# Operand tiles 32 bytes longer in a fused decoder block: the same instructions on other SBUF addresses

## The chip, the cores and the metric

The kernel runs on one NeuronCore of a Trainium2 chip. The metric is the device time of one execution in microseconds. A profiled execution gives a trace with the start and the duration of each instruction on TensorE (PE, with its weight loads shown apart as PEld), VectorE (DVE), ScalarE (ACT), GpSimd (POOL) and of each DMA.

## The reference

One decoder layer on x of 512 tokens by 1024 channels, all in float32:

```
h = rms_norm(x, g_mix);  p = h @ w_in              # 1024 -> 7680 columns
q, fp, iv, go, bg, cg, xc, u, v, gates = split(p)
o_a = hgrn2_mix(q, fp, iv, go)                     # gated linear recurrence, 4 heads of 128
o_b = short_conv_mix(bg, cg, xc)                   # 3-tap causal convolution
o_c = spatial_gating_mix(u, v)                     # 128 x 128 causal token mixing
merged = sum_n sigmoid(gate_n) * (o_n @ w_branch[n])
x = x + merged @ w_o
x = x + square(relu(rms_norm(x, g_ffn) @ w_ff1)) @ w_ff2   # 1024 -> 4096 -> 1024
return rms_norm(x, g_final)
```

## The kernel before, in words

Activations lie feature-major: a tile has 128 features on the partitions and the 512 tokens (`S`) along the free dimension, 2048 bytes per partition. Weights come in tiles of 128 by 1024 float32, 4096 bytes per partition, that is eight stationary blocks of 128 columns.

**Split operands.** Each large product is made of three matmuls in the float32r type. Every operand is split into a rounded part `hi` (an ACT copy) and the rest `lo` (a DVE subtraction), and `mm3` (L88 to L91) issues hi·hi (L89), hi·lo (L90) and lo·hi (L91) into one PSUM accumulator. Each of these matmuls has its own weight load of 128 columns, also where two in a row use the same block.

**Tiles.** Three helpers give out the SBUF tiles that these matmuls read: `xslot` (L55, 16 tiles of 128 by 512 for the input and later the second norm's input), `zslot` (L58, 24 tiles of 128 by 512: recurrence, branch inputs, hidden rows of the feed-forward, the residual) and `hslot` (L61, 16 tiles of 128 by 1024: the recurrence's work tiles, the merged rows, the second feed-forward weight). Each of these tags has one buffer. The split weights `wh` and `wl` (L83, L84, L744, L745, L795, L796) have three buffers each. The raw weight lands by DMA in `raw` (L74, three buffers). `tmp` (L113, six buffers of 2080 bytes) is for elementwise work, and `ones_r` (L105) is a constant block of ones.

**Order of the work.** The program's order is written out by hand. `proj` units (24 matmuls each: eight blocks of the contraction times three) give the input projection; `v_mm` (L403) makes the spatial gate's input with x stationary and the weight moving; the recurrence's small float32 matmuls (L317 and others, 128 columns) stand between the units; `branch` (L517) and `full` (L627) give the branch maps and the output projection. Then the feed-forward alternates: four units of `full` on the first weight (96 matmuls, moving operand x, stationary wh and wl), and `ff2_mm` of the group before (96 matmuls, moving operand z, stationary h). The last group is done in two token halves with 256-column matmuls (`fin_mm`, L897), and the final norm follows. In two ways there are other pairings: at the start x is stationary for the value rows (L833), and `ones_mm` (L144 to L146) sums over partitions with `ones_r` stationary and two `tmp` tiles moving; that happens three times.

Weights are prefetched: `issue` starts the DMA into `raw`, `split_hi` (L740) and `split_lo` make `wh` and `wl` (or two h tiles) one unit or more ahead of their matmuls.

Of the kernel before, what the change touches and what calls it, by code (L numbers as in the profile page):

```python
# [8 lines left out]
F32R = mybir.dt.float32r  # L9
# [4 lines left out]
P = 128  # L14
S = 512
# [21 lines left out]
def trunk_kernel(ctx: ExitStack, tc, xT, w_f, w_t, w_bc, w_a, w_o, w_1, w_2, vecs, rows, w_sg, cst, lmask, out):  # L37
    nc = tc.nc
    cp = ctx.enter_context(tc.tile_pool(name="cp", bufs=1))
    wp = ctx.enter_context(tc.tile_pool(name="wp", bufs=3))  # L40
    rp = ctx.enter_context(tc.tile_pool(name="rp", bufs=1))
# [6 lines left out]
    def nm(s):  # L48
        uid[0] += 1
        return f"{s}_{uid[0]}"  # L50

    def ct(shape, name, dt=F32):
        return cp.tile(shape, dt, name=name, tag=name)

    def xslot(i, dt):  # L55
        return rp.tile([P, S], dt, tag=f"x{i}", name=nm("x"))

    def zslot(i, dt):  # L58
        return rp.tile([P, S], dt, tag=f"z{i}", name=nm("z"))

    def hslot(i, dt):  # L61
        return rp.tile([P, 2 * S], dt, tag=f"h{i}", name=nm("h"))

    def acc():
        return pa.tile([P, S], F32, tag="acc", name=nm("acc"))
# [4 lines left out]
    def tt(e, o, a, b, op):  # L70
        return e.tensor_tensor(out=o, in0=a, in1=b, op=op)  # L71

    def raw():
        return wp.tile([P, 2 * S], F32, tag="raw", name=nm("raw"))  # L74

    def split(src, hi, lo):
        act.activation(hi, src, AF.Copy)
        tt(dve, lo, src, f(hi), ALU.subtract)

    def load_w(dram):  # L80
        r = raw()
        nc.sync.dma_start(r, dram)
        hi = wp.tile([P, 2 * S], F32R, tag="wh", name=nm("wh"))  # L83
        lo = wp.tile([P, 2 * S], F32R, tag="wl", name=nm("wl"))  # L84
        split(r, hi, lo)
        return hi, lo

# [5 lines left out]
    def cs(k, n=P):  # L93
        return slice(k * n, (k + 1) * n)

    # constants
    vec = ct([P, V_N], "vec")
    cons = ct([P, C_N], "cons")
    ident = cons[:, C_ID:C_ID + P]
# [13 lines left out]
        return wp.tile([P, w], dt, tag="tmp", name=nm("tmp"), bufs=6)  # L113

    def rsqrt_cols(src, n, inv, eps, dst):
        """dst[:, :n] = (src * inv + eps) ** -0.5"""
        a = wp.tile([P, 4], F32, tag="ra", name=nm("ra"), bufs=4)
        dve.tensor_scalar(out=a[:, :n], in0=src, scalar1=inv, scalar2=eps, op0=ALU.mult, op1=ALU.add)
        tt(pool, dst[:, :n], a[:, :n], mhalf[:, :n], ALU.pow)
# [49 lines left out]
    units = []  # L169
# [5 lines left out]
    loads, when = [], {}  # L175
# [14 lines left out]
            return a  # L190
        return unit(w_f[j], mm, ev)

    # recurrence: decays, keys, queries
    def ev_f(h, a):
        kk[h] = zslot(2 * h, F32)
        A[h] = zslot(2 * h + 1, F32)
        hs = [hslot(h * 4 + i, F32) for i in range(4)]
        names = ("QA", "t1", "QB", "y", "q", "R", "go", "att")
        d = {n: hs[i // 2][:, cs(i % 2, S)] for i, n in enumerate(names)}
        heads.append(d)  # L200
        fp = d["QA"]
        tt(dve, fp, a, rb, ALU.mult)
        act.activation(kk[h], fp, AF.Sigmoid, scale=-1.0)
        act.activation(d["t1"], fp, AF.Abs)
        pool.memset(d["att"], 0.0)
# [55 lines left out]
            dve.tensor_scalar(out=d["y"], in0=d["y"], scalar1=al[:, h:h + 1], scalar2=cl[:, h:h + 1], op0=ALU.add, op1=ALU.max)  # L261
            tt(dve, A[h], d["y"], d["t1"], ALU.add)

    # recurrence: interactions at distance scale m = 2 ** l
    def halves(ap, m):
        v = ap.rearrange("p (b two m) -> p b two m", two=2, m=m)
        if m == 1:
            v = v[:, :, :, 0]
            return v[:, :, 0], v[:, :, 1]
        return v[:, :, 0, :], v[:, :, 1, :]  # L270
# [51 lines left out]
            mk = lm[:, cs(l)].unsqueeze(1).to_broadcast([P, 4, P])  # L322
            dve.copy_predicated(v4(d["att"]), mk, v4(d["ps"]))

    # recurrence: blocks of 128 through the state
    def far_prep(pair):
        for h in pair:
            d = heads[h]
            act.activation(d["y"][:, :3 * P], d["R"][:, :3 * P], AF.Exp)
            act.activation(d["t1"][:, P:], A[h][:, P:], AF.Exp)  # L330
        for h in pair:
            d = heads[h]
            tt(dve, d["QA"][:, :3 * P], kk[h][:, :3 * P], d["y"][:, :3 * P], ALU.mult)
            tt(dve, d["QB"][:, P:], d["q"][:, P:], d["t1"][:, P:], ALU.mult)
# [64 lines left out]
            zt[0][h] = (zslot(2 * h, F32R), zslot(2 * h + 1, F32R))  # L399
            split(d["t1"], *zt[0][h])  # L400

    # spatial gate
    def v_mm(j):  # L403
        def mm(w):
            if j == 0:
# [73 lines left out]
        zt[2][g] = (zslot(16 + 2 * g, F32R), zslot(17 + 2 * g, F32R))  # L479
        split(part["sv", g], *zt[2][g])  # L480

    # short convolution
    def ev_cg(c, a):
        y = tmp()
        part["cy"] = y
        tt(dve, y, a, rb2, ALU.mult)
# [18 lines left out]
        yield  # L505
        tt(dve, lo, y, f(hi), ALU.subtract)

    # gates, branch outputs, merge
    def ev_gate(d, n, a):
        g = tmp()  # L510
        part[n] = g
        tt(dve, g, a, rb, ALU.mult)
        act.activation(g, g, AF.Sigmoid)
# [19 lines left out]
        tt(dve, mt[:, S:], part[0], f(mt[:, :S]), ALU.subtract)  # L533
        mg.append((mt[:, :S], mt[:, S:]))

    # order of the units of tensor work
    for h in range(NH):
        proj(4 + h, lambda a, h=h: ev_f(h, a))
    for h in range(NH):
# [57 lines left out]
        at(pre, 19 + g, sg_split, g)  # L597
    at(pre, 21, go_sig)

    # output projection, residual, second norm  # L600
    x2, x2h, x2l = [], [], []

    def reload_x():
# [37 lines left out]
        ones_mm(part["c2"], part["qh"], part["ql"])  # L641

    def ffn_rows():
        """-2 * (mean square + eps) ** -0.5, on every partition"""
        a, r, t = tmp(), tmp(), tmp()
        act.activation(r, part["c2"], AF.Sqrt, scale=1.0 / D, bias=eps_c)
        dve.tensor_scalar(out=a, in0=part["c2"], scalar1=1.0 / D, scalar2=EPS, op0=ALU.mult, op1=ALU.add)
        dve.reciprocal(r, r)
        tt(pool, t, a, r, ALU.mult)
        tt(pool, t, t, r, ALU.mult)  # L650
        part["r2b"] = ct([P, S], "rb2")
        dve.scalar_tensor_tensor(out=part["r2b"], in0=t, scalar=-3.0, in1=r, op0=ALU.add, op1=ALU.mult)
# [1 line left out]
    def ffn_late():  # L654
        return [ev_1(i, held[i]) for i in range(3)]

    # feed-forward
    hid = {}

    def ev_1(i, a):  # L660
# [67 lines left out]
    order = [x for s in sorted(when) for x in when[s]]  # L728
# [10 lines left out]
    def split_hi(i):  # L739
        _, n, tiles = loads[i]  # L740
        if tiles:
            hi, lo = (hslot(t, F32R) for t in tiles)
        else:
            hi = wp.tile([P, 2 * S], F32R, tag="wh", name=nm("wh"))  # L744
            lo = wp.tile([P, 2 * S], F32R, tag="wl", name=nm("wl"))  # L745
        act.activation(hi[:, :n], raws[i][:, :n], AF.Copy)  # L746
        ws[i] = (hi, lo)

# [4 lines left out]

    held = []
    with tc.manual_schedule():
        # warm the tensor engine's clock and the activation tables while the first loads run
        dve.memset(ones, 1.0)
        pool.memset(mhalf, -0.5)
        nc.scalar.dma_start(vec, vecs)
# [2 lines left out]
        warm = acc()  # L762
        for i in range(WARM):
            pe.matmul(warm[:, :P], ones, ones, start=True, stop=True)

        # x: load, scale by the gain, split, sum of squares; the recurrence's value rows, token-major
        xr = [zslot(k, F32) for k in range(KD)]
        rw = []
        for k in range(KD):
# [17 lines left out]
        for k in range(KD + 1):  # L787
            if k < KD:
                hi = xslot(2 * k, F32R)
                lo = xslot(2 * k + 1, F32R)  # L790
                xh.append(hi)
                xl.append(lo)
                g = vcol(V_GMIX + k)
                if k % 2 == 0:
                    wh = wp.tile([P, 2 * S], F32R, tag="wh", name=nm("wh"))  # L795
                    wl = wp.tile([P, 2 * S], F32R, tag="wl", name=nm("wl"))  # L796
                c = cs(k % 2, S)
                iw.append((wh[:, c], wl[:, c]))
                if k == 0:
                    dve.tensor_copy(wh[:, c], rw[k // 2][:, c])  # L800
                    pieces = (slice(0, 256), slice(256, 512))
                else:
                    pieces = (slice(0, 512),)
                for h in pieces:
                    act.activation(hi[:, h], xr[k][:, h], AF.Copy, scale=g)
                if k > 0:
                    act.activation(wh[:, c], rw[k // 2][:, c], AF.Copy)
                for h in pieces:
                    dve.scalar_tensor_tensor(out=lo[:, h], in0=xr[k][:, h], scalar=g, in1=f(hi[:, h]), op0=ALU.mult, op1=ALU.subtract)
                tt(dve, wl[:, c], rw[k // 2][:, c], f(wh[:, c]), ALU.subtract)  # L810
                if k == 0:
                    act.activation(sq_tot, xr[k], AF.Square)
                else:
                    sq = tmp()
                    act.activation(sq, xr[k], AF.Square)
                    tt(pool, sq_tot, sq_tot, sq, ALU.add)
            if k == KD:
                cps = acc()
                col_sums(cps, sq_tot)
                rsqrt_cols(cps[:, :4], 4, 1.0 / D, EPS, rstd)  # L820
                dg = diag(rstd)
                dh = ones_hi(dg)
                dl = ones_lo(dg, dh)
            j = k - 1
            if j < 0:
                continue
            hi, lo = xh[j], xl[j]
            wh_, wl_ = iw[j]
            for rnd in range(3):
                for t in range(4):  # L830
                    lh = (hi, hi, lo)[rnd][:, cs(t)]
                    rh = (wh_, wl_, wh_)[rnd]
                    pe.matmul(a4[t], lh, rh, start=j == 0 and rnd == 0, stop=j == KD - 1 and rnd == 2)  # L833
            if j in (3, 5, 6):
                issue()
            if j == 5:
                split_hi(order[0])
                split_lo(order[0])
# [52 lines left out]
                fn(*a)  # L891
        prev[0](prev[1])

        # last group of the feed-forward, by token halves, and the final norm
        g = NG - 1
        n2 = S // 2

# [75 lines left out]
        warm = acc()  # L973
# [60 lines left out]
```

## Time and profile before

| | |
|---|---|
| median of 3 runs | 860.64 us (859.86 to 861.35) |
| span of the profiled execution | 859.3 us |
| instructions in the span | 10105 |
| PE busy | 847.2 us, 99% |
| PEld busy | 706.8 us, 82% |
| DVE / ACT / POOL busy | 473.6 / 322.3 / 140.4 us |
| mean DMA rate | 97 GB/s |

The profiled execution is known by its span alone, from its first to its last instruction; what lies around the span in a timed run is the difference to the median, 1.3 us. A matmul's duration in the trace runs from its start to its modelled end and overlaps the next one, so the pace of PE is read from the starts of successive matmuls, not from their durations.

### The profile page before, as it was taken

To read this page: it belongs to the slowest core of one execution; us is meant where nothing else is said; L and a number is where in the kernel's file an instruction comes from. 1 tells how busy PE (TensorE), PEld (TensorE's weight loads), DVE (VectorE), ACT (ScalarE), POOL (GpSimd) and SP (SyncE) were. 2 spreads that over 40 slices of the span, in tenths; PEclk is the share of its full clock that TensorE was granted. 3 is DMA by queue.
4 is the path that set the end of the run, shared out by engine and by line. 5 is a ranking of instruction groups with operands and counts; after the bars stand their busy time and mean duration, and the time that the engine had idled before them with its cause. 6 is when DMAs were issued, how large, how long until landed. Compare 5 with 4: busy or idle time off the path is not lost.

```text
span 859.3 us, 10105 instructions
## 1 busy us (share of the span) xinstructions
PE 847.2 (99%) x3990; PEld 706.8 (82%) x3990; DVE 473.6 (55%) x623; ACT 322.3 (38%) x491; POOL 140.4 (16%) x152
## 2 busy tenths in 40 slices
PE   8999899999999999999999999999999999999997
PEld 7888788888888888888888888888888888888896
DVE  7456989978564444544445458444444444444424
ACT  6567355354333232323223446232232323232222
POOL 4313455661210000000001310000000000000034
PEclk9999999999999999999999999999999999999999
DMA  8331222212122323232235234222223232322002
GB/s 302 118 99 50 84 88 75 74 50 98 50 75 86 110 86 111 86 96 100 86 110 208 92 131 149 96 98 98 98 98 98 98 98 98 98 91 90 17 1 99
DMA packets 26256, 83.59 MB, mean 97 GB/s; under 512 B 3040, under 2 KB 3424, under 8 KB 26208
## 3 DMA queue, kind: packets, MB, share of 16 engines
q1 hardware_dynamic: 26064, 82.91, 29.1%
q8 instruction: 31, 0.51, 0.2%
q14 instruction: 17, 0.14, 0.1%
q10 hardware_dynamic: 144, 0.03, 0.0%
HBM read 80.83 MB, written 2.10 MB: 97 GB/s over the span
## 4 chain that ended last, share of the span: by engine, by line
PE 91%; DVE 3%; ACT 3%; issue 2%; DMA 0%; SPq 0%; POOL 0%; DVEq 0%; ACTq 0%
PE acc L89 28%; PE acc L91 28%; PE acc L90 28%; PE acc L317 3%; PE acc L833 1%; DVE wl L71 1%; DVE h L71 1%; ACT h L248 1%; DVE h L261 0%; DMA z<-xT 0%; ACT wh L746 0%; ACT h L252 0%; PE acc L469 0%; PE acc L370 0%; DVE h L298 0%
## 5 line engine op out<-in xcount | busy, mean ns | idle before, releaser
L89 PE MATMUL acc<-x,wh 128*128 128x512 f32 x672 | 265.5, 395 | 0.0
L90 PE MATMUL acc<-x,wh 128*128 128x512 f32 x672 | 262.7, 391 | 0.0
L91 PE MATMUL acc<-x,wl 128*128 128x512 f32 x672 | 262.7, 391 | 0.0
L746 ACT ACTIVATE wh<-raw 128x1024 fp32r<-128x1024 f32 (+1 forms) x112 | 115.0, 1028 | 377.0 <-PE acc L90 247.4
L71 DVE TENSOR_TENSOR wl<-raw,wh 128x1024 fp32r<-128x1024 f32 (+1 forms) x118 | 151.4, 1284 | 24.9 <-ACT wh L746 24.8
L91 PEld LDWEIGHTS acc<-x,wl 128*128 128x128 f32 x672 | 126.2, 188 | 28.6
L89 PEld LDWEIGHTS acc<-x,wh 128*128 128x128 f32 x672 | 126.3, 188 | 26.5
L90 PEld LDWEIGHTS acc<-x,wh 128*128 128x128 f32 x672 | 126.3, 188 | 26.4
L71 DVE TENSOR_TENSOR z<-z,acc 128x512 f32<-128x512 f32 (+1 forms) x80 | 50.6, 634 | 109.8 <-PE acc L91 109.8
L89 PE MATMUL acc<-z,h 128*128 128x512 f32 (+1 forms) x288 | 105.5, 366 | 0.0
L90 PE MATMUL acc<-z,h 128*128 128x512 f32 (+1 forms) x288 | 105.2, 365 | 0.0
L91 PE MATMUL acc<-z,h 128*128 128x512 f32 (+1 forms) x288 | 105.2, 365 | 0.0
L71 POOL TENSOR_TENSOR tmp<-tmp,tmp 128x512 f32<-128x512 f32 (+1 forms) x27 | 31.5, 1166 | 218.6 <-DVE tmp L71 186.9
L662 DVE SCALAR_TENSOR_TENSOR tmp<-acc,rb 128x512 f32<-128x512 f32 x32 | 21.9, 690 | 76.0 <-PE acc L91 76.0
L71 DVE TENSOR_TENSOR tmp<-acc,rb 128x512 f32<-128x512 f32 x28 | 19.3, 691 | 80.5 <-PE acc L91 80.5
L89 PEld LDWEIGHTS acc<-z,h 128*128 128x128 f32 x288 | 54.3, 189 | 8.8
L90 PEld LDWEIGHTS acc<-z,h 128*128 128x128 f32 x288 | 54.3, 189 | 8.8
L91 PEld LDWEIGHTS acc<-z,h 128*128 128x128 f32 x288 | 54.3, 189 | 8.7
L917 POOL TENSOR_SCALAR z<-z,vec 128x256 f32<-128x256 f32 x12 | 5.8, 484 | 312.5 <-ACT tmp L911 312.5
L663 ACT ACTIVATE tmp<-tmp 128x512 f32<-128x512 f32 x32 | 20.1, 628 | 69.2 <-DVE tmp L662 69.2
L71 DVE TENSOR_TENSOR h<-raw,h 128x1024 fp32r<-128x1024 f32 x32 | 38.9, 1217 | 0.0
L89 PE MATMUL acc<-z,wh 128*128 128x512 f32 x96 | 37.8, 394 | 0.0
(184 smaller groups left out, 984.4 us busy)
## 6 DMA issues: line engine op xcount, KB each, us to landing
raw<-w SPq DMA_DIRECT2D x64, 512.0 KB, 3.3
raw<-w_f SPq DMA_DIRECT2D x52, 512.0 KB, 3.3
raw<-w_bc SPq DMA_DIRECT2D x8, 512.0 KB, 3.3
raw<-w_o SPq DMA_DIRECT2D x8, 512.0 KB, 3.3
z<-xT SPq DMA_DIRECT2D x15, 256.0 KB, 4.3
raw<-w_t SPq DMA_DIRECT2D x4, 512.0 KB, 3.3
raw<-w_a SPq DMA_DIRECT2D x8, 256.0 KB, 2.5
out<-x SPq DMA_DIRECT2D x8, 256.0 KB, 2.1
```

The source lines that it names most:

```text
L71: return e.tensor_tensor(out=o, in0=a, in1=b, op=op)
L89: pe.matmul(o, lh, rh, start=start, stop=False)
L90: pe.matmul(o, lh, rl, start=False, stop=False)
L91: pe.matmul(o, ll, rh, start=False, stop=stop)
L248: act.activation(d["t1"], d["t1"], AF.Exp, scale=-1.0)
L317: pe.matmul(ps[:, cs(b)], kl[:, cs(b)], qk[:, cs(b)], start=True, stop=True)
L662: dve.scalar_tensor_tensor(out=t, in0=a, scalar=0.0, in1=part["r2b"], op0=ALU.max, op1=ALU.mult)
L663: act.activation(t, t, AF.Square, scale=0.5)
L746: act.activation(hi[:, :n], raws[i][:, :n], AF.Copy)
L833: pe.matmul(a4[t], lh, rh, start=j == 0 and rnd == 0, stop=j == KD - 1 and rnd == 2)
L917: pool.tensor_scalar(out=xv, in0=xv, scalar1=vcol(V_GFIN + d), scalar2=0.0, op0=ALU.mult, op1=ALU.add)
```

## The change

Every tile of `xslot`, `zslot`, `hslot`, `wh` and `wl` is allocated eight float32 elements longer and used without its last eight. Nothing else is changed (removed comments are left out of the diff):

```diff
     def xslot(i, dt):
-        return rp.tile([P, S], dt, tag=f"x{i}", name=nm("x"))
+        return rp.tile([P, S + 8], dt, tag=f"x{i}", name=nm("x"))[:, :S]
 
     def zslot(i, dt):
-        return rp.tile([P, S], dt, tag=f"z{i}", name=nm("z"))
+        return rp.tile([P, S + 8], dt, tag=f"z{i}", name=nm("z"))[:, :S]
 
     def hslot(i, dt):
-        return rp.tile([P, 2 * S], dt, tag=f"h{i}", name=nm("h"))
+        return rp.tile([P, 2 * S + 8], dt, tag=f"h{i}", name=nm("h"))[:, :2 * S]
...
-        hi = wp.tile([P, 2 * S], F32R, tag="wh", name=nm("wh"))
-        lo = wp.tile([P, 2 * S], F32R, tag="wl", name=nm("wl"))
+        hi = wp.tile([P, 2 * S + 8], F32R, tag="wh", name=nm("wh"))[:, :2 * S]
+        lo = wp.tile([P, 2 * S + 8], F32R, tag="wl", name=nm("wl"))[:, :2 * S]
```

The last two lines stand in the same form in `load_w`, `split_hi` and the opening loop. On all five engines the instructions, their order and their waits are the same in both programs. What moves is where the tiles start in each partition. From the two built programs, start address modulo 256 bytes:

| tiles | before | after |
|---|---|---|
| wh, 3 buffers | 32, 32, 32 | 32, 64, 96 |
| wl, 3 buffers | 32, 32, 32 | 128, 160, 192 |
| x, 16 tiles | 96, all | 96, 128, 160, 192, 224, 0, 32, 64, and again |
| z, 24 tiles | 96, all | all eight multiples of 32, in turn |
| h, 16 tiles | 96, all | all eight multiples of 32, in turn |
| raw, 3 buffers | 96, all | 96, all |
| tmp, 6 buffers | 96, 128, 160, 192, 224, 0 | the same |
| ones_r | 224 | 224 |

Each matmul's stationary block starts a multiple of 512 bytes into its tile, so it has its tile's offset. Of the 3345 places where one 512-column float32r matmul follows another, the distance from a moving tile to the next stationary one, modulo 256, was:

| distance | 0 | 32 | 64 | 96 | 128 | 160 | 192 | 224 |
|---|---|---|---|---|---|---|---|---|
| before | 675 | 0 | 189 | 1 | 4 | 0 | 2474 | 2 |
| after | 552 | 282 | 502 | 253 | 577 | 254 | 626 | 299 |

## Rows read from the trace of the kernel before

**Rows 1.** The page, busy time, share and instructions; granted clock in 40 slices.
```profile
PE 847.2 (99%) x3990; PEld 706.8 (82%) x3990; DVE 473.6 (55%) x623; ACT 322.3 (38%) x491; POOL 140.4 (16%) x152
...
PEclk9999999999999999999999999999999999999999
```

**Rows 2.** The chain that ended last: shares by engine; pieces (start us, us, what).
```profile
PE 91%; DVE 3%; ACT 3%; issue 2%; DMA 0%; SPq 0%; POOL 0%; DVEq 0%; ACTq 0%
...
1.63 3.82 DMA z<-xT
...
49.18 3.38 issue
...
96.27 1.96 PE acc L317 x8
```

**Rows 3.** Timeline of PE, second then first product, first matmuls: start us, us, instruction.
```profile
583.25 0.39 PE L89 MATMUL acc<-z,h 128*128 128x512 f32 x1
...
604.78 0.39 PE L91 MATMUL acc<-z,h 128*128 128x512 f32 x1
605.00 0.39 PE L89 MATMUL acc<-x,wh 128*128 128x512 f32 x1
...
626.98 0.39 PE L89 MATMUL acc<-z,h 128*128 128x512 f32 x1
```

**Rows 4.** Timeline of PE, v_mm: first and last of its first 72 matmuls.
```profile
74.99 0.39 PE L89 MATMUL acc<-wh,x 128*128 128x512 f32 x1
...
91.56 0.40 PE L91 MATMUL acc<-wh,x 128*128 128x512 f32 x1
```

**Rows 5.** Timeline of PE, last group: first and last of 120 half-width matmuls.
```profile
823.67 0.28 PE L89 MATMUL acc<-z,h 128*128 128x256 f32 x1
...
837.95 0.28 PE L91 MATMUL acc<-z,h 128*128 128x256 f32 x1
```

**Rows 6.** Timeline of PE around the three `ones_mm`, from first row to last.
```profile
35.35 0.40 PE L91 MATMUL acc<-x,wl 128*128 128x512 f32 x1
...
36.75 0.39 PE L89 MATMUL acc<-x,wh 128*128 128x512 f32 x1
...
57.81 0.40 PE L91 MATMUL acc<-x,wl 128*128 128x512 f32 x1
...
58.97 0.39 PE L91 MATMUL acc<-x,wl 128*128 128x512 f32 x1
...
505.64 0.39 PE L90 MATMUL acc<-x,wh 128*128 128x512 f32 x1
...
507.01 0.39 PE L91 MATMUL acc<-x,wl 128*128 128x512 f32 x1
```

**Rows 7.** Groups of matmuls by line: count, busy us, mean ns, idle before.
```profile
L89 PE MATMUL acc<-x,wh 128*128 128x512 f32 x672 | 265.5, 395 | 0.0
...
L89 PE MATMUL acc<-z,h 128*128 128x512 f32 (+1 forms) x288 | 105.5, 366 | 0.0
...
L89 PE MATMUL acc<-z,wh 128*128 128x512 f32 x96 | 37.8, 394 | 0.0
...
L89 PE MATMUL acc<-h,wh 128*128 128x512 f32 x64 | 25.2, 394 | 0.0
```

**Rows 8.** Groups by form, DVE then ACT, 510 to 820 us.
```profile
L71 DVE TENSOR_TENSOR h<-raw,h 128x1024 fp32r<-128x1024 f32 x30 | 36.5, 1217 | 0.0
L71 DVE TENSOR_TENSOR wl<-raw,wh 128x1024 fp32r<-128x1024 f32 x27 | 32.9, 1219 | 1.0 <-ACT wh L746 1.0
...
L746 ACT ACTIVATE h<-raw 128x1024 fp32r<-128x1024 f32 x30 | 31.4, 1045 | 0.0
L746 ACT ACTIVATE wh<-raw 128x1024 fp32r<-128x1024 f32 x27 | 28.5, 1056 | 128.9 <-PE acc L90 93.8 <-DMA raw<-w 35.0
```

**Rows 9.** The page, DMA issues: count, KB each, us to landing.
```profile
z<-xT SPq DMA_DIRECT2D x15, 256.0 KB, 4.3
```

More of the change, by code (lines that the diff above doesn't have):

```diff
@@ L743, in split_hi @@
         else:
-            hi = wp.tile([P, 2 * S], F32R, tag="wh", name=nm("wh"))
-            lo = wp.tile([P, 2 * S], F32R, tag="wl", name=nm("wl"))
+            hi = wp.tile([P, 2 * S + 8], F32R, tag="wh", name=nm("wh"))[:, :2 * S]
+            lo = wp.tile([P, 2 * S + 8], F32R, tag="wl", name=nm("wl"))[:, :2 * S]
         act.activation(hi[:, :n], raws[i][:, :n], AF.Copy)
@@ L794, in trunk_kernel @@
                 if k % 2 == 0:
-                    wh = wp.tile([P, 2 * S], F32R, tag="wh", name=nm("wh"))
-                    wl = wp.tile([P, 2 * S], F32R, tag="wl", name=nm("wl"))
+                    wh = wp.tile([P, 2 * S + 8], F32R, tag="wh", name=nm("wh"))[:, :2 * S]
+                    wl = wp.tile([P, 2 * S + 8], F32R, tag="wl", name=nm("wl"))[:, :2 * S]
                 c = cs(k % 2, S)
```

## The prediction

> **What bounds the kernel now.** I read the page first. TensorE is busy for 99% of the span at a granted clock of nine tenths or more in every slice, that is at its 2.4 GHz level; DVE is busy for 55%, ACT for 38% [rows 1]. The chain that ended last is PE for 91%, DVE and ACT for 3% each [rows 2]. Its pieces show where PE is not the limit: a DMA of x at the start (3.82 us), and the stretch from 49.18 us, where a wait of 3.38 us opens a chain of ACT and DVE work, to 96.27 us, where the first masked products (L317) get the chain back to PE. From there to the last group of the feed-forward the chain is matmul after matmul. So the time after about 104 us, and that before 49 us once the inputs are there, is the number of matmuls times the pace of PE.
>
> The pace comes from the timeline. A matmul's duration (395 or 366 ns [rows 7]) is a modelled latency and says nothing of it; the starts do. In the second feed-forward product 96 matmuls start between 583.25 and 604.78 us: 95 intervals in 21.53 us, **226.6 ns** each. In the next block, the first product, 96 intervals lie between 605.00 and 626.98 us: **229.0 ns** [rows 3]. In v_mm, 71 intervals between 74.99 and 91.56 us: **233.4 ns** [rows 4]. All three stream 512 columns, which takes 213.3 ns at 2.4 GHz, and all load 128 new columns each time. The 256-column matmuls of the last group have 119 intervals in 14.28 us, 120.0 ns [rows 5]. From 120.0 to 226.6 the extra 256 columns cost 106.6 ns, the full clock's rate, so about 13 ns of each matmul do not depend on its length, and 2 or 7 ns come on top in two of the three kinds.
>
> What differs between the kinds is where their operands lie. In the second product moving and stationary tiles both start at 96 modulo 256: distance 0, 226.6 ns. In the first product the moving tile is at 96 and the stationary at 32: distance 192, 229.0 ns. In v_mm it is the other way round: distance 64, 233.4 ns. This is a correlation over three kinds of code, but a change of offsets touches just this, and that makes it the question of the forecast.
>
> **The change part by part.** No instruction, wait or DMA is added, removed or moved. What changes is the start address of what PE, ACT, DVE, POOL and some DMAs read and write.
>
> *TensorE, the counts.* Matmuls at distance 192: three lines of 672, 96 and 64 [rows 7], 2,496; 110 of them run in the 49 to 104 us stretch where PE has slack, so 2,386 count. At distance 0: three lines of 288 [rows 7], 864, of which 192 are half width. At distance 64: v_mm, in the slack stretch, and the opening matmuls, which mostly wait for loads; both at nothing. If the offsets slow PE under the cover of 49 to 104 us, the 3 us in which PE waits there shrink first; 110 and 96 matmuls by 2 ns are 0.4 us.
>
> *TensorE, the new pace.* Afterwards the eight distances occur 253 to 626 times each, and they change from matmul to matmul. The trace has three distances in steady state; their mean is (226.6 + 229.0 + 233.4) / 3 = 229.7 ns. Of changing distances it has three samples, the three `ones_mm`, whose two moving tiles lie at 128 and 160, at 0 and 224, and at 0 and 96, with a stationary block at 224. Around the first, six intervals take 1.40 us; around the second, five take 1.16 us; around the third, six take 1.37 us [rows 6]. That is 3.93 us for 17, **231.2 ns** on average, where 17 at 229.0 ns are 3.89 us. If the 0.04 us are put down to the nine pairs in these samples whose distance is not the usual one, a changed pair costs about 4 ns more, 233 ns. I take the middle of 229.7, 231.2 and 233: 231.2 ns. Two of the three samples hold moving tiles at 0 and one holds one at 128, and none of their stretches is quicker than the block around it, so nothing shown speaks for a gain from a round address.
>
> The sum: 2,386 x (231.2 - 229.0) = 5.2 us; 672 x (231.2 - 226.6) = 3.1 us; 192 half-width matmuls by the same 4.6 ns, since the 13 ns showed themselves independent of length, 0.9 us. Together 9.2 us. The ends: if every pair ran at the best pace shown, 2,386 x 2.4 = 5.7 us less; if every one ran at the worst steady pace, 2,386 x 4.4 + 864 x 6.8 = 16.4 us more.
>
> *ACT, DVE and POOL.* The subtraction of a weight takes 1217 ns with operands at 96, 96 and 96 and 1219 ns with 96, 32 and 32; the ACT copy 1045 ns from 96 to 96 and 1056 ns from 96 to 32 [rows 8]. These engines hardly see the offset, so nothing. If that were wrong by 1%, the cover is their idle time (DVE 45%) except in the 49 to 104 us stretch, where 1% of it is half a microsecond.
>
> *DMA.* The weights land in `raw`, which does not move. The x tiles land in z tiles that do move (15 transfers, 4.3 us each to landing [rows 9]); on the chain they are the 3.82 us at the start [rows 2]. The trace has no such transfer to another offset. A tenth of 3.82 us either way is 0.4 us; I take nothing, because the transfer's size and form stay.
>
> The profiled span is 859.3 us, 1.3 us under the median of the timed runs; the same remainder is taken for the changed kernel. 859.3 + 9.2 + 1.3 = **869.8 us**.
>
> **A rule weighed against the trace.** Three distances and three paces [rows 3, 4] suggest that weight load and moving stream meet somewhere. The Trainium skill, "TensorE: Matmul & The Clock Gate", Part 2, step 1, says the opposite: TensorE has two independent SBUF read ports, and loading the next weights takes no read bandwidth from the running matmul. By it the sum would be 0. The rows do not refute it, since distance and kind of code change together in them. It is the first rival.
>
> **The rivals.**
>
> *1. Offsets do not matter; the paces belong to the kinds of code.* For it: in v_mm x is stationary and the weight moves, and in the second product the roles are played by h and z; distance is not the only difference. Against it: the branch maps and the output projection, with z and h moving and wh stationary, are other code at distance 192, and their matmuls show 394 ns, the same as the first product's 395 rather than the second's 366 [rows 7]. Then nothing changes: 860.6 us. Also the form in which the change does not do what it says: the offsets move, but PE never sees them. Chance 0.14.
>
> *2. The distance of 192 is a bad one, and the spread averages it away (the other side).* If most of the eight distances behave like 0, the 2,386 matmuls fall towards 226.6 ns and the second product keeps its pace: 5.7 us less, 854.9 us; half of it, 857.8 us. It decides at the point where the mean of the eight distances lies under about 228.5 ns, today's mean. For it: the best pace shown is one of three. Against it: both others and the samples lie above. Chance 0.14.
>
> *3. The 13 ns are themselves a collision of tiles that all start alike modulo 256.* Then a spread would remove part of it from most matmuls. All of it would be 2,386 x 15.7 + 864 x 13.3 = 49 us, 812 us; half, 836 us. For it: it is there at each length. Against it: it is no larger at distance 0 than at 64, and the samples at 0 and 128 are not quicker. Chance 0.07. By the rule of the same page's section "Back-to-back issue gap" a warm matmul costs its columns at 2.4 GHz plus 2.5 ns, an estimate of 215.8 ns for 512 columns; the trace shows 226.6 at best, so that page leaves about 11 ns unexplained, and a rival that removes it would end near this one's lower end.
>
> *4. Changing distances cost more than steady ones.* The first sample has 26 ns over 229.0 in six intervals with three changed pairs, near 9 ns a pair; at 237.7 ns for all, the time would be 859.3 + 30.4 + 1.3 = 891 us. Chance of over 880 us: 0.07.
>
> **How the numbers follow.** The forecast, that the mean distance is worse than the two distances of today, has 0.58, with a range of its own from 863 to 877 us (229.7 to 233.4 ns). About 0.2% is what a measurement of this kernel can tell from no change, here 1.7 us or 0.5 ns a matmul. Slower by more: 0.58 + 0.07 = 0.65. Within: 0.14. Faster by more: 0.14 + 0.07 = 0.21. The range goes from rival 2 at its full, with a margin for the start, 853 us, to 880 us, a little past the worst steady pace (877); it leaves out rival 3 and the upper part of rival 4.
>
> **What would show it.** In the changed profile the block of 96 matmuls of the second product should take longer than 21.53 us, about 22.0, and the first product's about 22.2 instead of 21.98, with intervals that vary from block to block with the buffer of wh. If both blocks keep their lengths to 0.05 us, rival 1 is right. If the first product's block shrinks to 21.75 us while the second's stays, rival 2 is; if intervals near 215 ns appear, rival 3 is. DVE's and ACT's mean durations should stay within 1%, PE busy at 98 to 99%. The forecast is wrong in its ground if the pace of a matmul in the changed kernel does not follow its distance at all.

## The result and the profile after

| | before | after |
|---|---|---|
| median | 861.0 us (859.86 to 862.09, 4 runs) | 870.92 us (870.11 to 871.11, 4 runs) |
| ratio | | 1.0112, 95% interval 1.0099 to 1.0126 |
| span of the profiled execution | 859.3 us | 868.3 us |

The changed kernel is 1.1% slower; 869.8 us was forecast, in a range from 853 to 880. The page of the changed kernel, where rows 1 stand for before:

```profile
PE 857.2 (99%) x3990; PEld 706.1 (81%) x3990; DVE 473.9 (55%) x623; ACT 322.8 (37%) x491; POOL 140.6 (16%) x152
...
PEclk9999999999999999999999999999999999999999
...
PE 93%; DVE 3%; ACT 3%; issue 1%; DMA 0%; SPq 0%; POOL 0%; DVEq 0%; ACTq 0%
...
z<-xT SPq DMA_DIRECT2D x15, 256.0 KB, 4.6
```

PE's busy time grew by 10.0 us and nothing else's by more than half a microsecond. The granted clock stayed at its upper level. The timeline of PE shows the new pace, first in the blocks that rows 3 show (second product, then first product), then in v_mm (rows 4) and in the half-width matmuls (rows 5); columns are start in us, duration in us, the instruction:

```profile
588.45 0.39 PE L89 MATMUL acc<-z,h 128*128 128x512 f32 x1
...
610.65 0.40 PE L89 MATMUL acc<-x,wh 128*128 128x512 f32 x1
...
632.93 0.39 PE L89 MATMUL acc<-z,h 128*128 128x512 f32 x1
```

```profile
74.56 0.39 PE L89 MATMUL acc<-wh,x 128*128 128x512 f32 x1
...
90.97 0.40 PE L91 MATMUL acc<-wh,x 128*128 128x512 f32 x1
...
832.89 0.28 PE L89 MATMUL acc<-z,h 128*128 128x256 f32 x1
...
847.04 0.28 PE L91 MATMUL acc<-z,h 128*128 128x256 f32 x1
```

96 matmuls of the second product take 22.20 us, 231.3 ns each (226.6 before); 96 of the first product 22.28 us, 232.1 ns (229.0). v_mm became quicker, 16.41 us for 71 intervals, 231.1 ns (233.4). The half-width matmuls also became a little quicker, 14.15 us for 119 intervals, 118.9 ns (120.0).

Where the microseconds went is read from three places in both timelines: the first matmul with x moving after the L317 products begin, the first matmul of the second product, and the first half-width one (823.67 us before [rows 5], 832.89 after, above). Before:

```profile
106.13 0.48 PE L89 MATMUL acc<-x,wh 128*128 128x512 f32 x1
...
539.51 0.39 PE L89 MATMUL acc<-z,h 128*128 128x512 f32 x1
```

After:

```profile
105.41 0.48 PE L89 MATMUL acc<-x,wh 128*128 128x512 f32 x1
...
543.98 0.39 PE L89 MATMUL acc<-z,h 128*128 128x512 f32 x1
```

From the first place to the second the kernel took 433.38 us and takes 438.57 (5.2 more); from there to the half-width matmuls 284.16 and 288.91 (4.75 more). That is 9.9 us, the difference of the medians. The spans of the two profiled executions differ by only 9.0: up to the first place the changed kernel's profile is 0.7 us ahead, because its first value-row matmul starts at 4.47 us and not at 5.69, and behind the third place it gains another 0.2. The early start belongs to the execution, not to the layout: the kernel of e4_p256 below has the old offsets modulo 256 and starts at 4.47 as well. Its x transfers also take 4.6 us to landing, so the step from 4.3 to 4.6 in the page above is not put down to the offsets.

The other engines kept their pace. DVE and ACT groups by form, 510 to 830 us, against rows 8:

```profile
L71 DVE TENSOR_TENSOR h<-raw,h 128x1024 fp32r<-128x1024 f32 x31 | 37.7, 1216 | 0.0
...
L71 DVE TENSOR_TENSOR wl<-raw,wh 128x1024 fp32r<-128x1024 f32 x28 | 34.2, 1220 | 3.6 <-ACT wh L746 3.6
...
L746 ACT ACTIVATE h<-raw 128x1024 fp32r<-128x1024 f32 x31 | 32.4, 1045 | 0.0
```

### The profile page after: what moved, and what is told of

Read it like the earlier page. It is cut to its first block, busy times and chain, and to the rows that moved or that the text cites. A ratio compares the mean times of both kernels' runs of the same rounds, so it can differ in the third digit from the quotient of the medians.

```text
span 868.3 us, 10105 instructions
## 1 busy us (share of the span) xinstructions
PE 857.2 (99%) x3990; PEld 706.1 (81%) x3990; DVE 473.9 (55%) x623; ACT 322.8 (37%) x491; POOL 140.6 (16%) x152
## 4 chain that ended last, share of the span: by engine, by line
PE 93%; DVE 3%; ACT 3%; issue 1%; DMA 0%; SPq 0%; POOL 0%; DVEq 0%; ACTq 0%
PE acc L89 28%; PE acc L90 28%; PE acc L91 28%; PE acc L317 3%; PE acc L833 3%; DVE wl L71 1%; DVE h L71 1%; ACT h L248 1%; DVE h L261 0%; ACT wh L746 0%; ACT h L252 0%; PE acc L469 0%; PE acc L370 0%; DMA z<-xT 0%; DVE h L298 0%
## 5 line engine op out<-in xcount | busy, mean ns | idle before, releaser
L89 PE MATMUL acc<-x,wh 128*128 128x512 f32 x672 | 266.5, 397 | 0.0
L90 PE MATMUL acc<-x,wh 128*128 128x512 f32 x672 | 264.6, 394 | 0.0
L90 PEld LDWEIGHTS acc<-x,wh 128*128 128x128 f32 x672 | 126.3, 188 | 28.8
L89 PEld LDWEIGHTS acc<-x,wh 128*128 128x128 f32 x672 | 126.2, 188 | 28.9
L89 PE MATMUL acc<-z,h 128*128 128x512 f32 (+1 forms) x288 | 106.3, 369 | 0.0
L90 PE MATMUL acc<-z,h 128*128 128x512 f32 (+1 forms) x288 | 106.2, 369 | 0.0
L89 PEld LDWEIGHTS acc<-z,h 128*128 128x128 f32 x288 | 54.1, 188 | 10.0
L90 PEld LDWEIGHTS acc<-z,h 128*128 128x128 f32 x288 | 54.1, 188 | 9.6
L71 DVE TENSOR_TENSOR tmp<-acc,tmp 128x512 f32<-128x512 f32 x32 | 22.0, 688 | 29.8 <-PE acc L91 29.8
```

What stands on the lines that cost most here:

```text
L89: pe.matmul(o, lh, rh, start=start, stop=False)
L90: pe.matmul(o, lh, rl, start=False, stop=False)
```

## The experiments

The theory: the distance modulo 256 between a moving tile and the next stationary one (or its own one; where a distance is held constant the two are the same) sets the pace of a float32r matmul; the change replaced a mild distance and the best one by a mixture of all eight. Its rivals: the pace belongs to the kind of code; the change of the distance from matmul to matmul costs by itself; a round start address helps.

All kernels but e1_d0 ran once, and single times of the kernel before lie between 857.9 and 862.1 us, so the paces inside the traces are compared rather than the spans. The mean granted clock was 0.994 to 0.999 in every run.

Most kernels are the one before with unused bytes ahead of a group of tiles, so that all tiles stay alike within a group and the distance is constant. For the first the edit is this line before L44; the others differ in the count (40 elements for e3_d32, 16 for e2_d128, 24 for e5_d96, 64 for e4_p256):

```diff
+    rp.tile([P, 48], F32, tag="pad", name="pad")
     dve, act, pool, pe = nc.vector, nc.scalar, nc.gpsimd, nc.tensor
```

**e1_d0, distance 0 everywhere.**

> The kernel before, with 192 unused bytes ahead of the x, z and h tiles, so that these start at 32 modulo 256 like wh and wl: distance 0 everywhere, all tiles still alike. If the distance between the moving tile and the next stationary one sets the pace: the first product, the projections, the branch maps and the output projection fall from 229.0 to 226.6 ns a matmul, the second product stays at 226.6, v_mm falls from 233.4 to 226.6; 2,386 x 2.4 ns = 5.7 us less, about 855 us, ratio 0.993. If the paces belong to the kinds of code: the same 229.0, 226.6 and 233.4 ns and the same time as before.

Measured: median 855.82 us (6 runs) against 861.14 (11 runs), ratio 0.994, interval 0.9926 to 0.9954. Its timeline, v_mm, then a block of the second product and one of the first (L90 here is L89 of before):

```profile
74.07 0.39 PE L90 MATMUL acc<-wh,x 128*128 128x512 f32 x1
...
90.17 0.39 PE L92 MATMUL acc<-wh,x 128*128 128x512 f32 x1
...
622.78 0.39 PE L90 MATMUL acc<-z,h 128*128 128x512 f32 x1
...
644.54 0.39 PE L90 MATMUL acc<-x,wh 128*128 128x512 f32 x1
...
666.30 0.39 PE L90 MATMUL acc<-z,h 128*128 128x512 f32 x1
```

Both blocks take 21.76 us, 226.7 ns a matmul, and v_mm 16.10 us for 71 intervals, 226.8 ns. Three kinds of code, one pace: the kind of code is not what separates them. This version beats both kernels.

**e2_d128, distance 128.**

> 64 unused bytes ahead of the x, z and h tiles (start 160 modulo 256), wh and wl at 32: distance 128 in the first product, held constant. If the distance sets the pace, and distances not yet seen are like those seen: between 226.6 and 233.4 ns in the first product, 226.6 in the second (distance 0 still). If it is the change of the distance from matmul to matmul that costs, every constant distance is cheap: 226.6 to 229. If it is the kind of code: 229.0.

Measured: span 867.2 us. A block of the first product runs from

```profile
655.04 0.40 PE L90 MATMUL acc<-x,wh 128*128 128x512 f32 x1
...
677.36 0.40 PE L90 MATMUL acc<-z,h 128*128 128x512 f32 x1
```

22.32 us, 232.5 ns; the second product stays at 227. A constant distance can cost more than the 229.0 ns of before, so the change of distance is not needed for the loss.

**e3_d32, distance 32, moving tiles at 0.**

> 160 unused bytes ahead of the x, z and h tiles (start 0 modulo 256), wh and wl at 32: distance 32, constant, all moving tiles at a round address. Distance: 226.6 to 233.4 ns in the first product, 226.6 in the second. Change of distance alone costs: at most 229. Round start of the moving tile helps (rival 3 of the prediction): under 226 ns in both products. Kind of code: 229.0 and 226.6.

Measured: span 868.6 us.

```profile
656.42 0.39 PE L90 MATMUL acc<-x,wh 128*128 128x512 f32 x1
...
678.82 0.39 PE L90 MATMUL acc<-z,h 128*128 128x512 f32 x1
```

22.40 us, 233.3 ns in the first product; v_mm, at distance 224 here, 71 intervals in 16.57 us, 233.4 ns. A round start of the moving tile gains nothing.

**e4_p256, the old offsets 256 bytes further on.**

> 256 unused bytes ahead of the x, z and h tiles: every start address modulo 256 is as before, distance 192 in the first product modulo 256 but not modulo 512. If only addresses modulo 256 count: 229.0, 226.6 and 233.4 ns, the time of before. If a longer period counts (512 or more): another pace in the first product, up to 4 ns away, and 226.6 in the second, where the distance stays 0.

Measured: span 860.2 us. A block of the first product takes 21.98 us (649.64 to 671.62 us), one of the second 21.76 us (to 693.38), as before to the hundredth. A shift by 256 bytes changes no pace. As 0 and 128 have different paces in the first product (226.7 and 232.5 ns), counting modulo 128 is not enough.

**e5_d96, distance 96, and 160 in v_mm.**

> 96 unused bytes ahead of the x, z and h tiles (start 192 modulo 256), wh and wl at 32: distance 96 in the first product and 160 in v_mm, both constant. If constant distances average to what the changed kernel shows (232.0 ns in its first product), these two, the last not yet measured, lie at 230 to 236 ns: with 226.7 at 0, 233.3 at 32, 64 and 224, 232.4 at 128 and 228.9 at 192 their mean has to be near 234 for a plain mean of 232. If the change of the distance from matmul to matmul is what costs, they lie at 229 or less. Second product 226.7 in both.

Measured: span 872.5 us, the slowest kernel of all.

```profile
659.81 0.39 PE L90 MATMUL acc<-x,wh 128*128 128x512 f32 x1
...
682.30 0.40 PE L90 MATMUL acc<-z,h 128*128 128x512 f32 x1
```

22.49 us, 234.3 ns at distance 96. In v_mm, at distance 160,

```profile
76.44 0.39 PE L90 MATMUL acc<-wh,x 128*128 128x512 f32 x1
...
93.01 0.40 PE L92 MATMUL acc<-wh,x 128*128 128x512 f32 x1
```

71 intervals take 16.57 us, 233.4 ns. With this all eight constant distances have a pace:

| distance | 0 | 32 | 64 | 96 | 128 | 160 | 192 | 224 |
|---|---|---|---|---|---|---|---|---|
| ns a matmul | 226.7 | 233.3 | 233.4 | 234.3 | 232.5 | 233.4 | 229.0 | 233.4 |
| measured in | first product | first product | v_mm | first product | first product | v_mm | first product | v_mm |

Each value comes from one kind of code and one stretch. At 128 the first product shows how far that matters: in e2_d128 its last 72 matmuls ahead of v_mm ran at

```profile
58.13 0.40 PE L90 MATMUL acc<-x,wh 128*128 128x512 f32 x1
...
74.93 0.40 PE L90 MATMUL acc<-wh,x 128*128 128x512 f32 x1
```

16.80 us for 72, 233.3 ns, and the same kind of matmul at 232.5 ns later. The three values from v_mm may therefore be a nanosecond high. The plain mean of the table is 232.0 ns. The changed kernel, which has all eight, shows 232.1 in the first product's block above; whether that is more than a coincidence is tested below. The kernel before had the two best, 0 and 192.

**e6_q16, distance 16.** wh and wl begin four elements into a buffer 64 elements longer, with 48 elements of padding as in e1_d0:

```diff
-        hi = wp.tile([P, 2 * S], F32R, tag="wh", name=nm("wh"))
-        lo = wp.tile([P, 2 * S], F32R, tag="wl", name=nm("wl"))
+        hi = wp.tile([P, 2 * S + 64], F32R, tag="wh", name=nm("wh"))[:, 4:4 + 2 * S]
+        lo = wp.tile([P, 2 * S + 64], F32R, tag="wl", name=nm("wl"))[:, 4:4 + 2 * S]
```

> wh and wl begin 16 bytes into a longer buffer (48 modulo 256, all six), x, z and h at 32: distance 16 in the first product, 240 in v_mm. If what counts is whether moving tile and stationary block start alike within 32 bytes or more: 226.7 ns in both. If the distance counts byte for byte, 16 lies between 226.7 (distance 0) and 233.3 (distance 32): 227 to 233 ns in the first product. A pace under 226.5 would mean that 0 is not the best distance.

Measured: span 857.2 us. In the same stage there are two paces. Six units after the second norm's `ones_mm` (144 matmuls), and a block behind the first stretch of the second product:

```profile
505.03 0.39 PE L90 MATMUL acc<-x,wh 128*128 128x512 f32 x1
...
538.62 0.39 PE L90 MATMUL acc<-z,h 128*128 128x512 f32 x1
...
560.41 0.39 PE L90 MATMUL acc<-x,wh 128*128 128x512 f32 x1
...
582.17 0.39 PE L90 MATMUL acc<-z,h 128*128 128x512 f32 x1
```

33.59 us for 144 is 233.3 ns, 21.76 us for 96 is 226.7 ns, with the same instructions at the same distance. Well ahead of that `ones_mm` the pace was the quick one:

```profile
278.81 0.39 PE L90 MATMUL acc<-x,wh 128*128 128x512 f32 x1
...
295.13 0.39 PE L90 MATMUL acc<-z,wh 128*128 128x512 f32 x1
```

16.32 us for 72 matmuls, 226.7 ns, and so on up to the `ones_mm`. At 16 the pace depends on what ran before: it became 233.3 ns behind the `ones_mm`, whose tiles have other offsets, and 226.7 again behind a stretch of the second product, at distance 0. Such a stretch is not the only way back: between 113 and 243 us, where the units stand between the recurrence's 128-column products, some ran at one pace and some at the other, and from 243 us up to the `ones_mm` all were quick. v_mm, at 240, ran at 231.6 ns.

**e7_abs0, distance 0 with all tiles at 0.** The padding is 48 elements ahead of x, z and h and 56 ahead of wh and wl.

> Distance 0 as in e1_d0, but all operand tiles (wh, wl, x, z, h) start at 0 modulo 256 and not at 32. If the distance alone counts: 226.7 ns in every product, the pace of e1_d0. If the round start saves a part of the 13 ns (rival 3 of the prediction): under 225 ns, and a span under 852 us.

Measured: span 853.6 us, 855.4 us in one run. Blocks of both products take 21.76 us each, 226.7 ns. At 0, 32 and 96 alike (here, in e1_d0, and in the second product of before) it does not matter where all tiles start as long as they start alike; the 13 ns stay.

**e8_rponly and e9_wponly, the change in two halves.** The first has the diff's lines of `xslot`, `zslot` and `hslot` alone, the second those of `wh` and `wl` alone.

> Only the x, z and h tiles are 32 bytes longer; wh and wl stay at 32. If a matmul costs what its distance costs when that is held constant (226.7 at 0, 233.3 at 32, 64, 160 and 224, 234.3 at 96, 232.4 at 128, 228.9 at 192), the counts of its distances give 231.4 ns in the first product and 230.8 in the second; 2,386 x 2.5 + 672 x 4.1 = 8.7 us over the kernel before, span about 868. If the change of distance costs by itself, above that in both products: here the distance changes with every moving tile.

Measured: span 868.0 us; a block of the first product, then one of the second:

```profile
655.11 0.39 PE L89 MATMUL acc<-x,wh 128*128 128x512 f32 x1
...
677.29 0.40 PE L89 MATMUL acc<-z,h 128*128 128x512 f32 x1
...
699.50 0.40 PE L89 MATMUL acc<-x,wh 128*128 128x512 f32 x1
```

22.18 us, 231.0 ns, and 22.21 us, 231.4 ns: 0.4 ns under the table's mean and 0.6 over it.

> Only wh and wl are 32 bytes longer; x, z and h all start alike (32). By the same table 231.9 ns in the first product and 226.7 in the second, 2,386 x 3.0 = 7.2 us over the kernel before, span about 866.5. If the second product's loss in the changed kernel came from anything but the offsets of its own h and z tiles, it shows here too.

Measured: span 864.6 us; again a block of each product:

```profile
652.79 0.40 PE L89 MATMUL acc<-x,wh 128*128 128x512 f32 x1
...
675.07 0.39 PE L89 MATMUL acc<-z,h 128*128 128x512 f32 x1
...
696.84 0.39 PE L89 MATMUL acc<-x,wh 128*128 128x512 f32 x1
```

First product 22.28 us, 232.1 ns, second 21.77 us, 226.8 ns. The span is 1.9 us under the expected one because this run reached the L317 products early; from the first matmul with x moving behind them to the half-width ones it lost 6.9 us against the kernel before, where 7.2 were expected. The second product's loss comes from its own tiles. In the first product the half with wh and wl does the whole harm (232.1 ns) and the half with x, z and h two thirds of it (231.0 against 229.0): one staggered side is enough to mix the distances.

**e10_split96, distances 0 and 96 mixed.** 24 elements of padding ahead of x, z and h, and 24 between wh and wl.

> wh, x, z and h at 32, wl at 128: distance 0 to wh and 96 to wl. By the table, one next stationary block in three is at 96: (2 x 226.7 + 234.3) / 3 = 229.2 ns in the first product. If it is the weight load that runs during a matmul (the next one's) that collides, the long intervals are those from the start of L90 to that of L91 (the load of wl runs there). If a matmul collides with its own stationary block, they are those from L91 to L89.

Measured: span 867.8 us, first product

```profile
655.67 0.39 PE L90 MATMUL acc<-x,wh 128*128 128x512 f32 x1
...
677.99 0.40 PE L90 MATMUL acc<-z,h 128*128 128x512 f32 x1
```

22.32 us, 232.5 ns: a miss, 3.3 ns over the table's mean. All three intervals are long, not one (659.62, 659.85, 660.08, 660.31 us and on: 0.23 us each), so this run does not tell whether the distance to a matmul's own stationary block or to the next one counts, and no other run here does. One other distance in three slows all three.

**e11_h96, distance 96 put into the quick product.**

```diff
+    hp = ctx.enter_context(tc.tile_pool(name="hp", bufs=1))
+    hp.tile([P, 24], F32, tag="pad", name="pad")
...
-        return rp.tile([P, 2 * S], dt, tag=f"h{i}", name=nm("h"))
+        return hp.tile([P, 2 * S], dt, tag=f"h{i}", name=nm("h"))
```

> The h tiles get a pool of their own and start at 192; x and z at 96, wh and wl at 32 as before: distance 96 in the second product and in the output projection, 192 in the first product as before. If the distance sets the pace whatever the code: 234.3 ns in the second product (226.7 before) and in the output projection (228.9 before), 229.0 in the first; 672 x 7.6 + 192 x 5.4 = 6.1 us, span about 865.5. If the second product is quick because of its code: 226.7 ns. The half-width matmuls, all at 96 here, tell their price: 120 ns if short matmuls do not see the distance, up to 127 if they do as the long ones.

Measured: span 866.2 us. Second product, first product, half-width matmuls:

```profile
630.37 0.39 PE L91 MATMUL acc<-z,h 128*128 128x512 f32 x1
...
652.86 0.40 PE L91 MATMUL acc<-x,wh 128*128 128x512 f32 x1
...
674.84 0.39 PE L91 MATMUL acc<-z,h 128*128 128x512 f32 x1
...
830.75 0.28 PE L91 MATMUL acc<-z,h 128*128 128x256 f32 x1
...
844.87 0.29 PE L93 MATMUL acc<-z,h 128*128 128x256 f32 x1
```

22.49 us, 234.3 ns in the second product, as at distance 96 in the first product of e5_d96; 21.98 us, 229.0 ns in the first, where nothing was changed. The output projection's 192 matmuls also ran at 234.3 ns (228.9 before). The half-width matmuls take 14.12 us for 119 intervals, 118.7 ns: what costs 7.6 ns at 512 columns gains 1.3 at 256.

**e12_mix16, distances 0 and 16 mixed.** Only wl starts at 48.

> wh, x, z and h at 32, wl at 48: the next stationary block is at distance 0, 16, 0 in turn, and each of the two runs at 226.7 ns when held constant. If the miss of e10_split96 (232.6 ns against 229.2) came from the change of the distance by itself: about 229 to 230 ns in the first product here too, span about 860. If it came from the distance of 96 reaching into the matmuls behind it: 226.7 ns, span about 855.

Measured: span 863.0 us. Neither answer alone:

```profile
511.01 0.39 PE L90 MATMUL acc<-x,wh 128*128 128x512 f32 x1
...
544.45 0.39 PE L90 MATMUL acc<-z,h 128*128 128x512 f32 x1
...
566.22 0.39 PE L90 MATMUL acc<-x,wh 128*128 128x512 f32 x1
...
587.98 0.39 PE L90 MATMUL acc<-z,h 128*128 128x512 f32 x1
```

232.2 ns in the first 144 matmuls, 226.7 ns in the block behind a pure stretch at distance 0. So what e10_split96 missed is not simply a price of the change of distance, since here the same change costs 5.5 ns a matmul or nothing. The pace depends on the distances and on the pace that the matmuls come from; constant distance 0 was quick in every run. What in the engine makes it so stays open.

**The mixture, matmul by matmul.** The trace keeps the program's order, so each interval of the changed kernel can be set beside the addresses in the built program. For 512-column matmuls from 242 us on, mean interval by the distance to the next stationary block (176 to 488 intervals each):

| distance | 0 | 32 | 64 | 96 | 128 | 160 | 192 | 224 |
|---|---|---|---|---|---|---|---|---|
| held constant, ns | 226.7 | 233.3 | 233.4 | 234.3 | 232.5 | 233.4 | 229.0 | 233.4 |
| in the mixture, ns | 231.7 | 232.2 | 231.4 | 231.2 | 233.1 | 233.7 | 230.3 | 231.3 |

Sorted by the distance to the own block instead, the means are 230.3 to 233.5, with 231.3 at distance 0. In the mixture a pair at distance 0 is 5 ns dearer than in a row of its like, and one at 96 is 3 ns cheaper. A matmul there does not pay the price of its own distance, so the agreement of 232.1 with the table's mean explains nothing by itself: the mixtures of 0 with 96 and of 0 with 16, whose table means are 229.2 and 226.7, came to 232.5 and 232.2 as well.

## Why the prediction was right

**What bounds the kernel** held: PE at its pace, and no other engine moved. The wait of PE inside the slack stretch, 3.2 us before, was 3.1 after. Blocks of about 22.0 and 22.2 us were foretold for the two products, and 22.20 and 22.28 came.

**Distance, not kind of code** was the forecast's ground, argued from three kinds of code; e1_d0 and e11_h96 showed it in both directions for constant distances. The Trainium skill, "TensorE: Matmul & The Clock Gate", Part 2, step 1, states that loading the next weights does not take SBUF read bandwidth from the running matmul. The forecast's reading of it, that offsets then change nothing, is not borne out here: the same instructions ran at 226.7 or 234.3 ns by the distance of the two operands alone. Whether it is read bandwidth that is lost no run here shows.

The second step of the forecast, that a mixture runs at a mean of its distances' paces, gave a number close to the measured one but is not what happened: in the changed kernel the pace of a matmul hardly follows its distance, by the table above. That comes close to the forecast's own sign of a wrong ground. The closeness is partly luck, and partly the work of the `ones_mm` samples, which were changing distances themselves.

**The terms of the sum.** The 2,386 matmuls at distance 192 were to cost 5.2 us at 231.2 ns. The first product's block shows 232.1 ns, and the two stretches above gained 5.2 and 4.75 us, of which the second product's seven blocks take 672 x 4.3 = 2.9 us at their mean of 231.0 ns; so from 106 us on this term measured 7.0 us, and the 82 matmuls ahead of 49 us add 0.2. It was 2 us short: 231.2 was the middle of three guesses, and the lowest, 229.7, came from three steady distances that held the two best of eight. The mean of changing distances, also 231.2, from 17 matmuls around the `ones_mm`, was the better guide. The second product was put at 3.1 us and measured 2.9. The forecast's own range for this, 863 to 877 us, has its lower end too low: by the same terms 229.7 ns gives 860.6 + 4.3, about 865.

The half-width term had the wrong sign: 0.9 us more was forecast, 192 x (118.9 - 120.0) = 0.2 us less was found. The step that failed there is "the 13 ns showed themselves independent of length": the 13 ns are, but what the distance adds is not.

Together 7.2 + 2.9 - 0.2 = 9.9 us, by medians 9.9 us, forecast 9.2; a term that was 2 us short and one that was 1.1 too long partly cancel. The rest around the span was 1.8 us in the changed kernel's profiled run (870.11 - 868.3), and it is 1.7 to 1.8 in runs of the kernel before whose span is on record (861.21 - 859.4); the 1.3 of the forecast set one run's span against the median of others. As the forecast in effect adds 9.2 to that median, this does not touch it.

**The rivals.** Rival 1 fell with e1_d0. Rival 2 had its condition stated, a mean of the eight distances under 228.5 ns; the mean is 232.0. Rival 3 fell with e3_d32 and e7_abs0: tiles at 0, alike or not, keep the 13 ns. Rival 4, that changing distances cost more than steady ones, is half true: e10_split96 and the slow stretches of e12_mix16 lie 3.3 and 5.5 ns over the mean of their steady paces, and in the change itself the pairs at distance 0 lie 5 ns over theirs. But e8_rponly, e9_wponly and the whole of the change come out near the table's mean, and its price of 237.7 ns never came: whole blocks of mixed distances ran at 230.5 to 232.5.

## What to carry to other kernels

When PE is the bound, read the starts of successive matmuls, not their durations: blocks of one shape with different paces, here 226.6 and 229.0 ns, point to something other than columns and clock. For 512-column float32r matmuls here, the best layout was the one in which moving and stationary tiles start alike modulo 256; 192 bytes of padding in one place gave 0.6% (e1_d0), while spreading the tiles, a remedy that sounds right for collisions, cost 1.1%. Before spreading, find out with one run per distance whether the present layout is among the good ones, and do not expect a mixture to run at the mean of its parts: with one block in three at another distance the whole product ran at 232.5 ns (e10_split96).

## What was not expected

- The distance works on 512 columns and on 256 columns with opposite sign: 226.7 and 234.3 ns for distance 0 and 96 at full width, 120.0 and 118.7 ns at half width.
- The same matmuls at the same distance of 16 bytes had two lasting paces in one execution, 233.3 and 226.7 ns (e6_q16).
- About 13 ns a matmul remain at the best distance (226.7 ns for columns that take 213.3); nothing tried here moved them.
